# Sums over weights in a Strassen product: from four VectorE operations to two adding transfers and two additions in place

## The chip, the cores and the metric

The kernel runs on one core of one Trainium2 chip. The metric is device time in microseconds (us), from the start to the end of one execution; lower is better. Five engines work side by side, each through its own queue in order: TensorE (PE, with its weight loads as PEld), VectorE (DVE), ScalarE (ACT), GpSimd (POOL) and SyncE (SP), which here issues every DMA transfer.

## The reference

Two layers over 512 tokens of width 2048, in float32. The first layer is an mLSTM with 8 heads, the second an attention layer with 16 heads over one shared K and V. Nearly all of the work is in large products of a token matrix with a weight matrix:

```python
proj = h @ w_in                      # mLSTM: 2048 x 20496
y = sigmoid(o) * ht * silu(z)
x = x + gate * rmsnorm(y @ w_out)    # 4096 x 2048
kv = hkv @ kv_w                      # shared K and V: 2048 x 4096
qz = h @ w_in                        # attention: query and gate, 2048 x 4096
x = x + gate * rmsnorm((o * silu(z)) @ w_out)
```

## The kernel before, in words

A float32 product is made of three passes in the float32r type: each operand is split into a high and a low part, and `mm3` (L225) issues high x high, high x low and low x high. `split` (L180) makes the parts: ScalarE casts to the high part, VectorE subtracts to get the low part.

Weights come as a stream. `stream` (L60) lists the order in which the blocks of 128 x 128 are needed, and the host lays the array `wst` out in that order, in pieces of up to 1024 columns. `wpiece` (L187) takes the next piece: it loads it to a tile `wr` (tag `raw`, two buffers) and splits it to `wh` and `wl` (three buffers each).

Some products use Strassen's scheme in Winograd's form on 2 x 2 blocks of 128 x 128 weights and halves of 256 tokens: seven products of half width in place of eight. `proj_s` (L265) does this for two columns of weight blocks, c1 and c2. A pair of inner blocks k is either a Strassen pair (`sk`) or a plain one (`nk`); `pair_pieces` (L50) puts them into pieces, and `seven` and `eight` inside `proj_s` issue the matmuls. Strassen pairs of a piece form groups: one or two groups of one pair each, or (for the keys, `merged`) one group of two pairs. `proj_s` serves:

- the query, key and gate columns of heads 4 to 7 of the first layer (L584, up to 5 of 8 pairs, pool `hq`, three buffers of `wsh` and `wsl`),
- the shared keys (L928, 6 to 8 of 8 pairs, merged, pool `zp`, two buffers),
- the queries and gates of the 16 attention heads (L972, 7 of 8 pairs, pool `kq`, three buffers).

The sums over the weights are made in `wpiece` (L202 to L210). A piece carries for each group four blocks. VectorE subtracts twice into a tile `ws` (tag "ws", two buffers), and once in place into the raw tile (L206 to L208). Then the raw tile, with the sum that was made in place, is split as a whole, and each `ws` of three block widths is split to `wsh` and `wsl`. Of the seven products four read their weights from `wh` and `wl`, three from `wsh` and `wsl`.

The sums over the tokens are made by `half_sums` (L324), `three_sums` (L338) and at L948, and the four partial sums in PSUM (D, C, A, B) are combined at L313 to L322.

The order on each queue is not written out: the tile framework's planner orders the instructions by priority and by when it expects each to be ready, and puts in the waits for data and for buffers. `wpiece` runs with a priority 300 instructions ahead of its place (`ahead`, L184), so that loads and splits run ahead of the matmuls as far as the buffers allow. A tile of a tag with n buffers can be written once the tile n places back has had its last reader.

An attention head in its turn runs `queries` (L967): four pieces, of which the first holds one Strassen pair and the plain pair and the other three hold two Strassen pairs each, as two groups. Before the third piece, `mid` (L1039) issues the value product of the head two back and the scores and softmax of the head one back (`mixed` L1026, `weights` L987); after the last piece follow the transposes (`flipped` L1008).

Of the kernel before, what the change touches and what calls it, by code (L numbers as in the profile page):

```python
# [15 lines left out]
P = 128  # L16
# [43 lines left out]
def stream():  # L60
# [72 lines left out]
def hybrid_trunk(ctx, tc, xT, xN, c, adaT, cols, wst, wg, ext, kc, out):  # L133
# [53 lines left out]
    def wpiece(mat, groups=(), pl=None, bufs=2, tbufs=2):  # L187
# [7 lines left out]
        wpos[:] = i + 1, at + P * n  # L195
        with tc.high_priority(ahead[0]):
            own = spare[0] and i % (RAW_BUFS + 1) == 0
            raw = (spare[0] if own else wp).tile([P, 1024], F32, tag="raw", name=f"wr{i}", bufs=1 if own else RAW_BUFS)[:, :n]
            nc.sync.dma_start(raw, wst[at : at + P * n].rearrange("(p n) -> p n", p=P))
            ts = []  # L200
            c0 = 0
            for j, ns in enumerate(groups):  # L202
                w = ns * P
                r = raw[:, c0 : c0 + 4 * w]
                t = pl.tile([P, 3 * w], F32, tag="ws", name=f"ws{i}_{j}", bufs=tbufs)
                nc.vector.tensor_tensor(t[:, : 2 * w], r[:, w : 3 * w], r[:, : 2 * w], op=ALU.subtract)  # L206
                nc.vector.tensor_tensor(r[:, w : 2 * w], t[:, w : 2 * w], r[:, :w], op=ALU.add)
                nc.vector.tensor_tensor(t[:, 2 * w :], r[:, 3 * w :], r[:, w : 2 * w], op=ALU.subtract)  # L208
# [56 lines left out]
    def proj_s(mat, xs, ss, f, z1, z2, name, pl, bufs, at={}, merged=False):  # L265
# [6 lines left out]
        for i, (sk, nk) in enumerate(pieces):  # L272
# [10 lines left out]
            def eight():  # L283
                b0 = 4 * sum(len(ks) for ks in sk)
# [5 lines left out]
            def seven(g, ks):  # L290
                ns = len(ks)
                b0 = 4 * sum(len(u) for u in sk[:g])
# [861 lines left out]
```

## Time and profile before

| | |
|---|---|
| time, median of 2 runs | 2856.45 us (2855.57 to 2857.32) |
| span of the profiled execution | 2852.6 us |
| instructions in it | 40697 |
| granted TensorE clock, mean | 0.993 |
| DMA traffic | 524.61 MB, 184 GB/s on average |

For the profiled execution there is its span, from the first to the last instruction on the core; no separate time of that execution is listed, and the span lies 3.9 us below the median of the runs. Stretches of the span in which `proj_s` runs: about 890 to 1530 us (heads 4 to 7 of the first layer, with the value products between), 1980 to 2150 us (shared keys) and 2236 to 2640 us (attention).

In the rows of the profile, a name such as `wsh<-ws` gives the tile written and the tiles read; L181 and L182 are the two instructions of `split`, L223 is every matmul; `xN` is a count. In the table by stretches each engine has its busy time and, in brackets, its instructions. A line with `<-` after a number names what the engine waited for.

### The profile page before, as it was taken

What the parts mean: (1) busy time and instruction counts of PE and PEld (TensorE: products, weight loads), DVE (VectorE), ACT (ScalarE), POOL (GpSimd) and SP (SyncE); (2) the same over time, 40 slices, a digit from 0 to 9 for tenths busy, and PEclk for the clock granted to TensorE, in tenths of its full rate; (3) what the DMA queues carried; (4) which work ended last, traced back from release to release, by engine and by line L of the source; (5) the groups of instructions that cost most, each with busy time, mean ns of one, the idle gap of its engine ahead of it and who ended that gap; (6) DMA issues with size and microseconds to landing.
All of it is one profiled execution on the core that took longest, in us unless ns stands there. A gap on an engine that the chain in (4) does not pass through costs nothing.

```text
span 2852.6 us, 40697 instructions
## 1 busy us (share of the span) xinstructions
PE 2796.1 (98%) x15308; PEld 2425.8 (85%) x15308; DVE 2074.9 (73%) x3680; ACT 1337.4 (47%) x2005; POOL 0.2 (0%) x4
## 2 busy tenths in 40 slices
PE   7999999999999999999999999999999999999798
PEld 5787888888888989989898888888998999999687
DVE  7986978778688766857766445567875899998425
ACT  4244524234234544545545445577334566666323
POOL 0000000000000000000000000000000000000000
PEclk9999999999999999999999999999999999999899
DMA  8875687878764232332325657787336433333534
GB/s 298 301 245 185 232 308 247 296 236 279 260 236 132 93 115 97 108 100 100 104 96 168 205 197 241 232 285 259 137 137 210 141 126 117 121 126 123 184 104 173
DMA packets 177117, 524.61 MB, mean 184 GB/s; under 512 B 18788, under 2 KB 36228, under 8 KB 176408
## 3 DMA queue, kind: packets, MB, share of 16 engines
q1 hardware_dynamic: 176920, 522.01, 54.1%
q8 instruction: 120, 1.97, 0.3%
q14 instruction: 77, 0.63, 0.1%
HBM read 488.33 MB, written 38.85 MB: 185 GB/s over the span
## 4 chain that ended last, share of the span: by engine, by line
PE 86%; DVE 6%; DMA 4%; ACT 2%; issue 1%; SPq 0%; DVEq 0%; ACTq 0%
PE ps_y L223 18%; PE ps_v L223 10%; PE ps_o L223 5%; PE ps_z L223 5%; PE ps_azo L223 4%; PE ps_qk L223 4%; PE ps_kv L223 4%; PE ps_bzo L223 3%; PE ps_az L223 3%; PE ps_l L223 3%; PE ps_cz L223 2%; PE ps_dz L223 2%; PE ps_czo L223 2%; PE ps_dzo L223 2%; PE ps_s L223 2%; PE ps_bz L223 2%
## 5 line engine op out<-in xcount | busy, mean ns | idle before, releaser
L181 ACT CAST wh<-wr 128x1024 fp32r<-128x1024 f32 (+3 forms) x586 | 585.1, 1000 | 860.0 <-PE ps_y L223 210.0
L182 DVE TENSOR_TENSOR wl<-wr,wh 128x1024 fp32r<-128x1024 f32 (+3 forms) x586 | 678.5, 1160 | 421.5 <-ACT wh L181 416.7
L223 PE MATMUL ps_y<-wh,y 128*128 128x512 f32 x1536 | 478.6, 392 | 10.6 <-ACT wh L181 6.0
L223 PEld LDWEIGHTS ps_y<-wh,y 128*128 128x128 f32 x1536 | 289.9, 189 | 72.1 <-ACT wh L181 6.2
L223 PE MATMUL ps_v<-wh,h 128*128 128x512 f32 x1024 | 321.6, 390 | 0.4 <-DVE cv L529 0.4
L223 PE MATMUL ps_y<-wl,y 128*128 128x512 f32 x768 | 300.6, 391 | 0.0
L181 ACT CAST wsh<-ws 128x384 fp32r<-128x384 f32 (+1 forms) x253 | 138.4, 547 | 321.5 <-issue 127.3
L223 PEld LDWEIGHTS ps_v<-wh,h 128*128 128x128 f32 x1024 | 192.3, 188 | 40.5 <-issue 1.2
L182 DVE TENSOR_TENSOR wsl<-ws,wsh 128x384 fp32r<-128x384 f32 (+1 forms) x253 | 151.5, 599 | 99.8 <-ACT wsh L181 98.3
L223 PE MATMUL ps_v<-wl,h 128*128 128x512 f32 x512 | 199.8, 390 | 0.0
L381 DVE CUSTOM_DVE_ANT_0 ada<-ada,scB,cl 128x1024 f32<-128x1024 f32 x128 | 163.7, 1280 | 25.7 <-DMA ada<-in_adaT 25.6
L381 DVE CUSTOM_DVE_ANT_0 ada<-ada,scB,mod 128x1024 f32<-128x1024 f32 x128 | 163.9, 1280 | 19.9 <-DMA ada<-in_adaT 18.4
L223 PEld LDWEIGHTS ps_y<-wl,y 128*128 128x128 f32 x768 | 145.0, 189 | 30.6 <-DVE wl L182 0.9
L223 PE MATMUL ps_kv<-wh,hkv 128*128 128x512 f32 x512 | 159.3, 391 | 0.0
L206 DVE TENSOR_TENSOR ws<-wr 128x256 f32<-128x256 f32 (+1 forms) x253 | 112.2, 451 | 34.9 <-DMA wr<-in_wst 31.8
L223 PE MATMUL ps_qk<-h,wh 128*128 128x512 f32 x384 | 119.2, 390 | 0.0
L223 PE MATMUL ps_o<-h,wh 128*128 128x512 f32 x384 | 118.2, 389 | 0.0
L223 PE MATMUL ps_z<-h,wh 128*128 128x512 f32 x384 | 118.2, 389 | 0.0
L223 PEld LDWEIGHTS ps_v<-wl,h 128*128 128x128 f32 x512 | 96.2, 188 | 19.8 <-issue 0.9
L223 PEld LDWEIGHTS ps_kv<-wh,hkv 128*128 128x128 f32 x512 | 95.7, 188 | 19.5
L223 PE MATMUL ps_l<-h,wh 128*128 128x512 f32 x320 | 99.4, 392 | 1.3 <-ACT q L467 0.5
L223 PE MATMUL ps_kv<-wl,hkv 128*128 128x512 f32 x256 | 99.9, 390 | 0.1
(385 smaller groups left out, 5916.0 us busy)
## 6 DMA issues: line engine op xcount, KB each, us to landing
wr<-in_wst SPq DMA_DIRECT2D x520, 512.0 KB, 3.7
ada<-in_adaT SPq DMA_DIRECT2D x256, 512.0 KB, 5.9
xt<-nsc SPq DMA_DIRECT2D x46, 256.0 KB, 4.3
yr<-ysc SPq DMA_DIRECT2D x16, 512.0 KB, 4.3
wr<-in_wst SPq DMA_DIRECT2D x30, 256.0 KB, 4.0
wr<-in_wst SPq DMA_DIRECT2D x16, 384.0 KB, 5.8
bsc<-in_ext SPq DMA_DIRECT2D x16, 320.0 KB, 6.2
xt<-in_xT SPq DMA_DIRECT2D x4, 1024.0 KB, 7.0
```

Source lines behind the costliest of these rows:

```text
L181: nc.scalar.copy(hi, src)
L182: nc.vector.tensor_tensor(lo, src, hi.bitcast(F32), op=ALU.subtract)
L206: nc.vector.tensor_tensor(t[:, : 2 * w], r[:, w : 3 * w], r[:, : 2 * w], op=ALU.subtract)
L223: nc.tensor.matmul(ps, a, b, start=start, stop=stop)
L381: pin(nc.vector.tensor_tensor_reduce(at, at, scB[:, j * D // 2 : (j + 1) * D // 2], 1.0, mod[:, i : i + 1] if j else col(CB + i), ALU.mult ...
```

## The change

The sums are given other signs, so that all four over the weights are additions. A group's blocks in the stream are now three (0,c1), (1,c2), (1,c1), and the fourth, (0,c2), stands at the end of the piece. Two sums are made by transfers: a tile t (tag "ws") of two block widths gets the first two blocks by a load on SP's queue, and the fourth block is then added to both by a transfer with `accum_op` on GpSimd's queue, which reads it from the array twice. The piece itself is loaded without the fourth block. After the piece has been split, VectorE makes the other two sums by adding in place into the raw tile, and t and these two are split separately into the halves of one `wsh` and one `wsl` of four block widths. So three products read the piece's own blocks from `wh` and `wl`, and four read `wsh` and `wsl`. The buffers: `ws` has as many as `wsh` (three in the first layer, two for the keys and in attention, where before it had two everywhere), `wsl` at most two, and attention's `wsh` two for three. The sums over the tokens and the evacuation of PSUM change signs only.

```diff
     def tile_s(mat, c1, c2, f, merged=False):
         for sk, nk in pair_pieces(f, merged):
-            blocks = [(2 * k + i, c, P) for ks in sk for i, c in ((0, c1), (0, c2), (1, c2), (1, c1)) for k in ks]
-            out.append((mat, blocks + [(2 * k + i, c, P) for k in nk for i in range(2) for c in (c1, c2)]))
+            blocks = [(2 * k + i, c, P) for ks in sk for i, c in ((0, c1), (1, c2), (1, c1)) for k in ks]
+            blocks += [(2 * k + i, c, P) for k in nk for i in range(2) for c in (c1, c2)]
+            out.append((mat, blocks + [(2 * k, c2, P) for ks in sk for k in ks]))
...
-    def wpiece(mat, groups=(), pl=None, bufs=2, tbufs=2):
+    def wpiece(mat, groups=(), pl=None, bufs=2):
...
+        m = n - P * sum(groups)
         with tc.high_priority(ahead[0]):
             own = spare[0] and i % (RAW_BUFS + 1) == 0
-            raw = (spare[0] if own else wp).tile([P, 1024], F32, tag="raw", name=f"wr{i}", bufs=1 if own else RAW_BUFS)[:, :n]
-            nc.sync.dma_start(raw, wst[at : at + P * n].rearrange("(p n) -> p n", p=P))
+            raw = (spare[0] if own else wp).tile([P, 1024], F32, tag="raw", name=f"wr{i}", bufs=1 if own else RAW_BUFS)[:, :m]
+            src = wst[at : at + P * n].rearrange("(p n) -> p n", p=P)
             ts = []
-            c0 = 0
+            c0, c1 = 0, m
             for j, ns in enumerate(groups):
                 w = ns * P
-                r = raw[:, c0 : c0 + 4 * w]
-                t = pl.tile([P, 3 * w], F32, tag="ws", name=f"ws{i}_{j}", bufs=tbufs)
-                nc.vector.tensor_tensor(t[:, : 2 * w], r[:, w : 3 * w], r[:, : 2 * w], op=ALU.subtract)
-                nc.vector.tensor_tensor(r[:, w : 2 * w], t[:, w : 2 * w], r[:, :w], op=ALU.add)
-                nc.vector.tensor_tensor(t[:, 2 * w :], r[:, 3 * w :], r[:, w : 2 * w], op=ALU.subtract)
-                ts.append(t)
-                c0 += 4 * w
-            hi = wp.tile([P, 1024], F32R, tag="hi", name=f"wh{i}")[:, :n]
-            lo = wp.tile([P, 1024], F32R, tag="lo", name=f"wl{i}")[:, :n]
+                t = pl.tile([P, 2 * w], F32, tag="ws", name=f"ws{i}_{j}", bufs=bufs)
+                nc.sync.dma_start(t, src[:, c0 : c0 + 2 * w])
+                nc.gpsimd.dma_start(
+                    t.rearrange("p (a b) -> p a b", a=2),
+                    src[:, c1 : c1 + w].unsqueeze(1).to_broadcast([P, 2, w]),
+                    accum_op=ALU.add,
+                )
+                ts.append((t, raw[:, c0 + w : c0 + 3 * w]))
+                c0 += 3 * w
+                c1 += w
+            nc.sync.dma_start(raw, src[:, :m])
+            hi = wp.tile([P, 1024], F32R, tag="hi", name=f"wh{i}")[:, :m]
+            lo = wp.tile([P, 1024], F32R, tag="lo", name=f"wl{i}")[:, :m]
             split(hi, lo, raw)
             out = [(hi, lo)]
-            for j, t in enumerate(ts):
-                sh = pl.tile(list(t.shape), F32R, tag="wsh", name=f"wsh{i}_{j}", bufs=bufs)
-                sl = pl.tile(list(t.shape), F32R, tag="wsl", name=f"wsl{i}_{j}", bufs=bufs)
-                split(sh, sl, t)
+            for j, (t, r) in enumerate(ts):
+                w = groups[j] * P
+                nc.vector.tensor_tensor(r[:, :w], t[:, :w], r[:, :w], op=ALU.add)
+                nc.vector.tensor_tensor(r[:, w:], r[:, :w], r[:, w:], op=ALU.add)
+                sh = pl.tile([P, 4 * w], F32R, tag="wsh", name=f"wsh{i}_{j}", bufs=bufs)
+                sl = pl.tile([P, 4 * w], F32R, tag="wsl", name=f"wsl{i}_{j}", bufs=min(bufs, 2))
+                split(sh[:, : 2 * w], sl[:, : 2 * w], t)
+                split(sh[:, 2 * w :], sl[:, 2 * w :], r)
                 out.append((sh, sl))
         return out
...
-                    (D, h1_, 0, 1, lambda k: ss[k][1], False),
+                    (D, h1_, 1, 2, lambda k: ss[k][1], False),
                     (D, h0, 0, 0, lambda k: xs[2 * k][:, :, h0], end),
                     (C, h0, 1, 1, lambda k: ss[k][2], False),
                     (C, h1_, 1, 0, lambda k: ss[k][0], end),
-                    (A, h0, 0, 3, lambda k: xs[2 * k + 1][:, :, h0], False),
-                    (A, h1_, 1, 2, lambda k: xs[2 * k + 1][:, :, h1_], end),
-                    (B, h0, 0, 2, lambda k: ss[k][3], end),
+                    (A, h0, 0, 2, lambda k: xs[2 * k + 1][:, :, h0], False),
+                    (A, h1_, 1, 3, lambda k: xs[2 * k + 1][:, :, h1_], end),
+                    (B, h0, 0, 1, lambda k: ss[k][3], end),
...
-        proj_s("b_w_in", h2, h2s, ATT_PAIRS, z[:, 0:2, :], z[:, 2:4, :], f"z{h}", kq, 3, {2: mid})
+        proj_s("b_w_in", h2, h2s, ATT_PAIRS, z[:, 0:2, :], z[:, 2:4, :], f"z{h}", kq, 2, {2: mid})
```

The first product of `seven` (D, h1_) read the piece's split before; now it reads the group's.

More of the change, by code (lines that the diff above doesn't have):

```diff
@@ L283, in eight @@
             def eight():
-                b0 = 4 * sum(len(ks) for ks in sk)
+                b0 = 3 * sum(len(ks) for ks in sk)
                 for m, k in enumerate(nk):
@@ L327, in half_sums @@
         nc.vector.tensor_tensor(a11, a11, a21, op=ALU.subtract)
-        nc.vector.tensor_tensor(a21, a21, a22, op=ALU.add)
-        nc.vector.tensor_tensor(a22, a22, a11, op=ALU.subtract)
+        nc.vector.tensor_tensor(a21, a21, a22, op=ALU.subtract)
+        nc.vector.tensor_tensor(a22, a22, a11, op=ALU.add)
         nc.vector.tensor_tensor(a12, a12, a22, op=ALU.subtract)
@@ L341, in three_sums @@
         nc.vector.tensor_tensor(a11, a11, a21, op=ALU.subtract)
-        nc.vector.tensor_tensor(a22, a22, a11, op=ALU.subtract)
+        nc.vector.tensor_tensor(a22, a22, a11, op=ALU.add)
         nc.vector.tensor_tensor(a12, a12, a22, op=ALU.subtract)
@@ L947, in hybrid_trunk @@
         if k // 2 < ATT_PAIRS:
-            nc.vector.tensor_tensor(raw[0][:, 256:], raw[0][:, 256:], raw[1][:, 256:], op=ALU.add)
+            nc.vector.tensor_tensor(raw[0][:, 256:], raw[0][:, 256:], raw[1][:, 256:], op=ALU.subtract)
             h2s[k // 2][0] = h2[k][:, :, 256:]
```

8 lines of the change are left out of this document (4 added, 4 removed).

## The prediction

> **What bounds the kernel now.** I read the engine totals first, then the table by stretches of time, the chain that ended last, the waits, and the timeline of one attention head.
>
> ```profile
> span 2852.6 us, 40697 instructions
> PE 2796.1 (98%) x15308; PEld 2425.8 (85%) x15308; DVE 2074.9 (73%) x3680; ACT 1337.4 (47%) x2005; POOL 0.2 (0%) x4
> PE 86%; DVE 6%; DMA 4%; ACT 2%; issue 1%; SPq 0%; DVEq 0%; ACTq 0%
> ```
>
> PE is busy 98% of the span and makes 86% of the chain. The diff touches only the three stretches in which `proj_s` runs: gate and query/key projections of heads 4 to 7, the shared keys, the 16 attention heads. Columns: busy us and count of PE, PEld, DVE, ACT, POOL, granted clock, DMA share, GB/s.
>
> ```profile
> 890.00:1530.00 640.00, 636.68 (x3933) 575.58 (x3932) 455.38 (x861) 314.06 (x440) 0.00 (x0) 1.00 0.30 103
> 1980.00:2150.00 170.00, 165.45 (x1315) 162.33 (x1314) 135.90 (x225) 69.10 (x87) 0.00 (x0) 0.98 0.42 144
> 2250.00:2600.00 350.00, 348.75 (x2625) 333.23 (x2624) 317.61 (x843) 224.00 (x418) 0.00 (x0) 1.00 0.37 122
> ```
>
> PE stands still for 3.3, 4.6 and 1.3 us there: 9.2 us together. The change issues the same matmuls, so it cannot gain more than about 9 us (0.3%), whatever it takes off VectorE (DVE), which is 91% busy in the attention stretch but ends nothing there. The question is only what new waits it makes.
>
> The pace follows from two stretches of 50 us, one nearly all half-width products and one all of 512 columns:
>
> ```profile
> 2050.00:2100.00 50.00, 50.00 (x419) 50.00 (x418) 40.27 (x63) 18.44 (x22) 0.00 (x0) 1.00 0.38 137
> 2700.00:2750.00 50.00, 50.00 (x222) 41.40 (x221) 14.90 (x15) 13.20 (x19) 0.00 (x0) 1.00 0.34 119
> L313 ACT COPY z<-ps_dz x16: 358/366/375, 2255.3 to 2635.5; 128x256 f32<-128x256 f32 x16
> ```
>
> A half-width matmul takes 50/419 = 0.119 us, a full one 50/222 = 0.225. `seven` (21 half-width) is 2.5 us of PE and `eight` (12 full) 2.7. In attention, piece 0 (one Strassen group, one plain pair) is 5.2 us and pieces 1 to 3 (two groups each) 5.0. The evacuation of D marks heads: (2635.5-2255.3)/15 = 25.35 us each, for 7 groups; some 5 us are attention itself.
>
> **The change part by part.** *VectorE and ScalarE.* Rows of the attention stretch, by form (busy us, mean ns):
>
> ```profile
> L182 DVE TENSOR_TENSOR wl<-wr,wh 128x1024 fp32r<-128x1024 f32 x56 | 68.5, 1224 | 14.9 <-ACT wh L181 14.3
> L181 ACT CAST wh<-wr 128x1024 fp32r<-128x1024 f32 x56 | 58.6, 1046 | 36.4 <-DVE wr L207 34.8 <-DVE mx L1003 1.6
> L182 DVE TENSOR_TENSOR wsl<-ws,wsh 128x384 fp32r<-128x384 f32 x98 | 54.1, 553 | 9.0 <-ACT wsh L181 7.7
> L181 ACT CAST wsh<-ws 128x384 fp32r<-128x384 f32 x97 | 49.3, 508 | 51.9 <-PE ps_az L223 40.6 <-ACT z L313 8.0 <-DVE ws L206 1.8
> L206 DVE TENSOR_TENSOR ws<-wr 128x256 f32<-128x256 f32 x98 | 41.2, 421 | 1.2
> L208 DVE TENSOR_TENSOR ws<-wr 128x128 f32<-128x128 f32 x98 | 27.9, 285 | 0.9
> L207 DVE TENSOR_TENSOR wr<-ws,wr 128x128 f32<-128x128 f32 x97 | 27.0, 279 | 0.5
> L181 ACT CAST pt<-ps_t 128x256 fp32r<-128x256 f32 x13 | 5.1, 392 | 0.0
> ```
>
> Before, DVE spends per head 4 x 1.224 on the main split and 7 x (0.421 + 0.279 + 0.285 + 0.553) on groups: 15.7 us. After, the main split has 896 columns once and 768 three times (1.09 and 0.96 us, on the line between the 256- and 1024-column rows), and a group has two adds of 0.28 and two splits of 0.42: 4.0 + 9.8 = 13.8. That frees 1.9 us of DVE per head, 30 us in 16 heads, and is worth nothing, since DVE ends no PE wait of size there. ScalarE (ACT) gains instructions: 7 x 2 x 0.392 for 7 x 0.508, less on the main cast: about 1.2 us more per head, at 64% busy, costed at nothing; the main cast no longer waits for the sum in place (L207, 34.8 us above), a wait that PE does not see. If that cover were gone it would cost 19 us.
>
> The turned signs at the evacuation and in `half_sums` and `three_sums` keep every shape and count: nothing.
>
> *Traffic.* A pair now moves 7 blocks of 64 KB (2 in t, 2 added, 3 in raw) for 4: in attention 112 x 192 KB, about 54 GB/s on top of 122, with the DMA engines at a share of 0.37. SP issues one transfer more per group, at 0.33 us. Hidden by idle DMA engines and by a queue that mostly waits for slots; no price.
>
> *The new chain.* This is the term that counts. A tile t (tag ws) is now loaded, then added to by a second transfer that GpSimd (POOL) issues only once the load has landed, then read by the first add and by its split. Its slot is freed only then. In attention there are two slots for 7 groups a head, as there are now two for wsh and wsl instead of three. So a slot is used 3.5 times per head, and a head cannot be shorter than 3.5 C, with C the time from the issue of one load into a slot to that of the next. Behind the waiting load on SP stand the raw load of its piece, the next head's keys and values, the bias and the y2c store; behind POOL's transfer only the next addition; behind the add on DVE all of the softmax, for which the transposes and value products on PE wait.
>
> C is load + addition + work + hand-offs. Transfers and queues:
>
> ```profile
> wr<-in_wst SPq DMA_DIRECT2D x20, 128.0 KB, 2.6
> xt<-nsc SPq DMA_DIRECT2D x16, 128.0 KB, 4.7
> wr<-in_wst SPq DMA_DIRECT2D x30, 256.0 KB, 4.0
> wr<-in_wst SPq DMA_DIRECT2D x56, 512.0 KB, 3.3
> L961 SPq DMA_DIRECT2D kv<-ksc x16: 326/327/433, 2147.2 to 2599.3; - x16
> ```
>
> Start us, length us and engine of three casts and the subtractions that follow them:
>
> ```profile
> 2404.20 0.51 ACT L181 CAST wsh<-ws 128x384 fp32r<-128x384 f32 x1 [1.99 <-PE ps_az L223]
> 2405.13 0.55 DVE L182 TENSOR_TENSOR wsl<-ws,wsh 128x384 fp32r<-128x384 f32 x1
> ...
> 2406.72 0.52 ACT L181 CAST wsh<-ws 128x384 fp32r<-128x384 f32 x1 [0.49 <-ACT z L313]
> 2408.39 0.55 DVE L182 TENSOR_TENSOR wsl<-ws,wsh 128x384 fp32r<-128x384 f32 x1
> ...
> 2415.81 0.51 ACT L181 CAST wsh<-ws 128x384 fp32r<-128x384 f32 x1 [1.15 <-PE ps_az L223]
> 2416.35 0.56 DVE L182 TENSOR_TENSOR wsl<-ws,wsh 128x384 fp32r<-128x384 f32 x1 [0.59 <-ACT wsh L181]
> ```
>
> The load: 2.6 us, the row of 128 KB from the same array. Work: two adds and one split, 0.28 + 0.28 + 0.42 = 1.0. A hand-off to a busy in-order engine: the three casts end 0.42, 1.15 and 0.03 us before their subtraction starts, a half on average; two of them, 1.0. The addition: no row shows a transfer issued by POOL, nor one that adds. From below it takes what a plain load of as many bytes takes, 2.6; from above I bound it by the slowest load of 128 KB, 4.7. A gain is excluded. It moves two runs of 512 bytes per partition, reads both sides and is issued by software, so it is nearer the upper row: I take 4.0.
>
> C = 2.6 + 4.0 + 1.0 + 1.0 = 8.6; a head is 3.5 x 8.6 = 30.1 us for 25.35: 4.75 x 16 = **76 us**. With 2.6 for the addition C is 7.2 and a head 25.2: nothing. With 4.7, C is 9.3, a head 32.6: 115 us.
>
> The Trainium skill speaks for the lower end: "DMA: Bandwidth & Descriptors", section "Anatomy of one DMA — SWDGE (gpsimd) path", puts such a DMA at a fixed 2.0 us plus its bytes at 436 GB/s. By that the addition is an estimated 2.3 us, C 6.9, a head 24.2, and the sum would be no change; no run here shows it so far.
>
> *Two buffers of wsh for three.* The cast of a group now waits for PE's last read of the group two back. From there PE has 0.36 + 2.5 us of products before it needs the result; casts and subtractions of a group take about 2. Hidden by one group of PE work; with that gone, up to 0.5 us x 112 groups = 56 us, inside the range.
>
> *Shared keys.* 29 of the 32 groups are merged, with 256 KB per load; a slot is used every second piece, 10 us.
>
> ```profile
> L206 DVE TENSOR_TENSOR ws<-wr 128x512 f32<-128x512 f32 x29 | 19.9, 685 | 1.4 <-DMA wr<-in_wst 0.9 <-DVE zk L314 0.4
> ```
>
> C: load 4.0, addition 4.0, two adds of 256 columns and a split of 512 (0.42 + 0.42 + 0.68), hand-offs 1.0: 10.5. Over by 0.5 per two pieces: 29 x 0.25 = **7 us**, between 0 (addition 2.6) and 18 (4.7).
>
> *Heads 4 to 7 of the first layer.* 109 groups, three slots. Five groups take 3 x 5.2 + 5.0 = 20.6 us, so a slot has 12.4 us for C = 8.6. Hidden by 3.8 us of PE work per slot; with two slots it would be 2.5 x 8.6 = 21.5 us for every five groups, 0.9 us over, some 20 us in all.
>
> **Sum.** Against the profiled execution: 2852.6 + 76 + 7 = 2935.6. Its span lies 3.9 us under the median of the runs (2856.45), so the forecast is **2939.5 us**.
>
> **The rivals.**
>
> 1. *The chain is hidden (2857 us).* Place: the two slots of ws in attention. If the addition lands like a plain load, 3.5 C is at most 25.35, that is C at most 7.24, and PE sets the pace as before; the gain is at most 9 us. For it: 512 KB land in 3.3 us in that stretch, DMA engines are 63% idle, POOL does nothing else, and the 5 us of attention products per head let slots catch up. Against it: a two-group piece uses both slots in 5.0 us of PE, less than any C above, so each head has to catch up what three such pieces lose. The estimate from the Trainium skill above falls here.
>
> 2. *SP's order makes raw late (3002 us).* The program issues a piece's raw load behind its t loads. If the planner leaves it there, raw waits for the last slot of t as well: issue 0.33, raw 3.3, cast 0.83, subtraction 0.96, adds and splits of two groups 2.4, hand-offs 1.0 = 8.8 for each two-group piece, and 7.6 for piece 0: 34 us per head, 8.65 x 16 = 138, and 7 for the keys. For it: SP is one queue in order. Against it: DVE's work is interleaved instruction by instruction in the timeline, so the order follows expected readiness, and raw's slot frees earlier.
>
> 3. *VectorE holds POOL off (3025 us).* If making the addition's descriptors has to wait out one VectorE instruction, at most the 1.22 us of a main split, the addition is 5.2 us, C 9.8, a head 34.3: 143 us, and 25 in the keys.
>
> ```profile
> L1004 DVE TENSOR_SCALAR s<-s,mx 128x512 f32<-128x512 f32 x13 | 6.2, 480 | 0.0
> L1004 DVE TENSOR_SCALAR s<-s,mx 128x384 f32<-128x384 f32 x13 | 5.4, 414 | 0.0
> ```
>
> For it: DVE is 91% busy. Against it: only the scaling at L1004 runs at a faster rate per column (480-414 ns for 128 columns, 0.52 ns each, where the splits take (1224-421)/768 = 1.05), four short instructions a head.
>
> The Trainium skill ("SBUF — State Buffer", section "Who interferes with whom") says that a VectorE instruction in a 2-port mode shuts GpSimd out of writing descriptors, and infers that tensor_tensor does not. By that rule only L1004 could delay an addition, by under 0.5 us a head, 8 us in all; the trace before cannot show it.
>
> **How the numbers follow.** Chain exposed, my forecast: 0.48, of which 0.10 lies within 2% (addition under some 3.7 us). Hidden: 0.31. Raw late: 0.12. POOL held off: 0.08. A gain above 2% is excluded by the 9 us; 0.01 is left for it. About 2% is what a measurement of this kernel tells from no change. So faster 0.01, within 2% 0.31 + 0.10 = 0.41, slower 0.38 + 0.12 + 0.08 = 0.58. The forecast's own range is 2870 to 2990 (addition 3.0 to 4.7); taking in the hidden case below and the two dear ones above gives 2850 to 3030.
>
> **What would show it.** Right: heads in attention about 30 us apart at the evacuation of D; PE's idle time in the `proj_s` products with wsh or wh as operand, released by DVE splits, which in turn waited for a DMA into ws; 253 DMA issues on POOL landing in about 4 us; the first layer's heads unchanged near 640 us for their stretch; DVE some 30 us less busy in attention. Wrong: heads still at 25.35 us (rival 1); DVE waiting for wr rather than ws (rival 2); POOL's transfers much slower beside DVE's work than in gaps (rival 3); or PE losing its time in the first layer, where I see three slots as cover.

## The result and the profile after

The changed kernel takes 3099.68 us (median of 2 runs, 3094.99 to 3104.37), against 2856.45 before: a ratio of 1.0855, 95% interval 1.0835 to 1.0876. That is 243 us slower. The forecast was 83 us slower, so the sign was right and the size was a third of what came; the time lies above the range.

The page of the changed kernel: its span, engine totals, its two queues of data, and the chain that ended last, by engine and by line.

```profile
span 3093.2 us, 42385 instructions
PE 2877.2 (93%) x15308; PEld 2474.4 (80%) x15308; DVE 2000.0 (65%) x3680; ACT 1372.3 (44%) x2258; POOL 305.1 (10%) x257
q1 hardware_dynamic: 213352, 540.51, 53.4%
q0 software_dynamic: 68816, 36.98, 9.4%
PE 57%; DMA 21%; DVE 10%; issue 6%; ACT 5%; SPq 0%; POOLq 0%; ACTq 0%; DVEq 0%; POOL 0%
DMA ws<-in_wst 16%; PE ps_y L233 16%; PE ps_v L233 9%; PE ps_o L233 4%; PE ps_z L233 4%; PE ps_qk L233 3%; PE ps_kv L233 3%; PE ps_l L233 3%; DMA wr<-in_wst 3%; PE ps_azo L233 2%; DVE wl L183 2%; PE ps_lead L233 2%; DVE wsl L183 2%; PE ps_bzo L233 1%; ACT wh L182 1%
```

DVE lost 75 us of work in the whole kernel and PE fell from 98% busy to 93%. DMA, 4% of the chain before, is now 21% of it, and transfers into ws are 16%. The same three stages as stretches, each a little longer than before since it takes longer now (columns: length, busy and count of PE, PEld, DVE, ACT, POOL, clock, DMA share, GB/s):

```profile
890.00:1600.00 710.00, 668.31 (x3999) 591.99 (x3998) 432.55 (x875) 337.23 (x562) 127.59 (x106) 0.99 0.50 126
2050.00:2240.00 190.00, 167.03 (x1268) 161.95 (x1267) 115.01 (x210) 70.43 (x112) 33.72 (x28) 0.95 0.68 172
2330.00:2880.00 550.00, 448.86 (x2994) 413.62 (x2992) 335.09 (x960) 270.54 (x588) 130.15 (x108) 0.93 0.54 128
```

PE stands idle in all three, 42, 23 and 101 us, where it stood 1 to 5 us before. To see how much each stage costs I use the evacuations of D (L313 before, L323 after) as milestones, from the view of one source line (first and last start in us):

```profile
L323 ACT COPY zo<-ps_dzo x16: 365/373/373, 917.5 to 1579.2; 128x256 f32<-128x256 f32 x16
L323 ACT COPY z<-ps_dz x16: 366/372/376, 2351.1 to 2875.4; 128x256 f32<-128x256 f32 x16
L323 ACT COPY zk<-ps_dk x8: 349/367/369, 2062.3 to 2235.3; 128x256 f32<-128x256 f32 x8
```

Before, the rows of zo and zk are these; that of z stands in the prediction:

```profile
L313 ACT COPY zo<-ps_dzo x16: 373/373/373, 919.6 to 1524.2; 128x256 f32<-128x256 f32 x16
L313 ACT COPY zk<-ps_dk x8: 348/374/374, 2002.5 to 2146.0; 128x256 f32<-128x256 f32 x8
```

Up to the last zo the kernel is 55.0 us late; to the last zk another 34.3 (656.1 for 621.8 us from the one milestone to the other); from there to the last z another 150.6 (640.1 for 489.5). The three make 240 of the 240.6 us by which the span grew. A head of attention takes (2875.4 - 2351.1)/15 = 34.95 us, where 30.1 was forecast and 25.35 stood before.

The waits in attention (2330 to 2880 us; engine, line, waited for: total us, times, longest):

```profile
DVE wr L223 <- DMA ws<-in_wst: 129.0, 57, 5.3
ACT wsh L182 <- DMA ws<-in_wst: 97.1, 50, 6.7
ACT wh L182 <- DMA wr<-in_wst: 36.5, 27, 4.4
PE ps_dz L233 <- ACT wsh L182: 33.1, 24, 3.5
PE ps_dz L233 <- DVE wsl L183: 28.7, 25, 4.1
```

PE waits for the halves of the sums (wsh, wsl; 62 of its 101 us), and those wait for a DMA into ws. The raw tile (wr) is late too, but less. The transfers themselves, from issue to landing (KB each, median us):

```profile
ws<-in_wst SPq DMA_DIRECT2D x224, 128.0 KB, 2.5
ws<-in_wst POOLq DMA_DIRECT2D x224, 128.0 KB, 3.8
ws<-in_wst SPq DMA_DIRECT2D x29, 256.0 KB, 3.0
ws<-in_wst POOLq DMA_DIRECT2D x29, 256.0 KB, 4.9
```

So in the median the transfers of 128 KB cost what the prediction took for them, 2.5 and 3.8 us for 2.6 and 4.0; the mean of the additions in attention is 4.2. What is longer is the rest of a slot's round. I took from the trace, for each use of a slot of ws, the starts of its load, of its POOL transfer, of its first reader, the end of its last reader and the start of the next load into it (attention without its first head; medians need not add up):

| stage (slots) | load to POOL | POOL to first read | first read to release | release to next load | round |
|---|---|---|---|---|---|
| first layer (3), median | 3.07 | 5.41 | 6.46 | 0.07 | 15.54 |
| keys (2), mean | 4.03 | 5.94 | 2.52 | 0.05 | 12.54 |
| attention (2), mean | 3.25 | 4.33 | 2.40 | 0.03 | 10.01 |

In all three a slot is loaded again as soon as it is free, and so 3.5 x 10.01 is 35.0 us, the head. That would hold for any buffer that is refilled at once; that the slots set the pace in attention is told by the waits above and by the experiments. By position in a head the seven rounds in attention last 9.3, 10.0, 8.8, 8.3, 8.4, 12.9 and 12.4 us. Five are near the forecast's 8.6; the two of the last piece, next to the softmax, are 4 us longer. One of them, in lines from the timelines of SP, POOL and DVE (start, length, engine, line, operation, count, and in brackets the idle time before it and what ended it):

```profile
2503.52 5.28 SPq L207 DMA_DIRECT2D ws<-in_wst  x2
2507.25 1.20 POOL L208 DMA_DIRECT2D ws<-in_wst  x1 [4.07 <-DVE wr L224]
2511.11 0.29 DVE L223 TENSOR_TENSOR wr<-ws,wr 128x128 f32<-128x128 f32 x1 [1.53 <-issue]
2511.93 1.20 POOL L208 DMA_DIRECT2D ws<-in_wst  x1 [3.48 <-DVE mx L1011]
2517.89 0.29 DVE L223 TENSOR_TENSOR wr<-ws,wr 128x128 f32<-128x128 f32 x1 [3.72 <-DMA ws<-in_wst]
2518.10 1.09 DVE L183 TENSOR_TENSOR wl<-wr,wh 128x896 fp32r<-128x896 f32 x1
2519.10 0.42 DVE L183 TENSOR_TENSOR wsl<-ws,wsh 128x256 fp32r<-128x256 f32 x1
2519.55 0.33 SPq L207 DMA_DIRECT2D ws<-in_wst  x1
```

The first slot's load starts at 2503.52 (the line holds the second slot's load too, at 2508.47), its addition at 2507.25, its first reader at 2511.11. Its last reader is the split at 2519.10. That split stands on DVE behind the first add of the second slot (2517.89), and this add waits 3.72 us for the second slot's addition, issued at 2511.93. So one slot is held by the transfer into the other, and the next load goes out only at 2519.55: 16.0 us a round. In the last piece of a head this order of the two stands in 8 of 16 heads, in the second and third pieces in none. Where it stands, the round of the first slot averages 15.0 us; in the other heads 10.4.

### The profile page after: what moved, and what is told of

The parts are those of the page before. It is cut to its first block, busy times and chain, and to the rows that moved or that the text cites. A ratio compares the mean times of both kernels' runs of the same rounds, so it can differ in the third digit from the quotient of the medians.

```text
span 3093.2 us, 42385 instructions
## 1 busy us (share of the span) xinstructions
PE 2877.2 (93%) x15308; PEld 2474.4 (80%) x15308; DVE 2000.0 (65%) x3680; ACT 1372.3 (44%) x2258; POOL 305.1 (10%) x257
## 3 DMA queue, kind: packets, MB, share of 16 engines
q0 software_dynamic: 68816, 36.98, 9.4%
## 4 chain that ended last, share of the span: by engine, by line
PE 57%; DMA 21%; DVE 10%; issue 6%; ACT 5%; SPq 0%; POOLq 0%; ACTq 0%; DVEq 0%; POOL 0%
DMA ws<-in_wst 16%; PE ps_y L233 16%; PE ps_v L233 9%; PE ps_o L233 4%; PE ps_z L233 4%; PE ps_qk L233 3%; PE ps_kv L233 3%; PE ps_l L233 3%; DMA wr<-in_wst 3%; PE ps_azo L233 2%; DVE wl L183 2%; PE ps_lead L233 2%; DVE wsl L183 2%; PE ps_bzo L233 1%; ACT wh L182 1%
## 5 line engine op out<-in xcount | busy, mean ns | idle before, releaser
L183 DVE TENSOR_TENSOR wl<-wr,wh 128x1024 fp32r<-128x1024 f32 (+4 forms) x586 | 641.2, 1096 | 501.6 <-ACT wh L182 492.0
L182 ACT CAST wh<-wr 128x1024 fp32r<-128x1024 f32 (+4 forms) x586 | 554.9, 948 | 901.5 <-PE ps_y L233 207.9
L208 POOL DMA_DIRECT2D ws<-in_wst x253 | 304.9, 1213 | 2562.2 <-DVE h1r L338 875.8
L182 ACT CAST wsh<-ws 128x256 fp32r<-128x256 f32 (+1 forms) x253 | 108.6, 429 | 388.8 <-DMA ws<-in_wst 247.8
L223 DVE TENSOR_TENSOR wr<-ws,wr 128x128 f32<-128x128 f32 (+1 forms) x253 | 75.5, 304 | 222.8 <-DMA ws<-in_wst 155.9
L183 DVE TENSOR_TENSOR wsl<-ws,wsh 128x256 fp32r<-128x256 f32 (+1 forms) x253 | 114.1, 451 | 64.9 <-PE ps_azo L233 40.7
L182 ACT CAST wsh<-wr 128x256 fp32r<-128x256 f32 (+1 forms) x253 | 106.7, 427 | 101.2 <-DVE wr L224 100.4
L183 DVE TENSOR_TENSOR wsl<-wr,wsh 128x256 fp32r<-128x256 f32 (+1 forms) x253 | 114.1, 451 | 28.6 <-ACT wsh L182 25.7
```

The costliest lines, as they stand in the source:

```text
L182: nc.scalar.copy(hi, src)
L183: nc.vector.tensor_tensor(lo, src, hi.bitcast(F32), op=ALU.subtract)
L208: nc.gpsimd.dma_start(t.rearrange("p (a b) -> p a b", a=2), src[:, c1 : c1 + w].unsqueeze(1).to_broadcast([P, 2, w]), accum_op=ALU.add,)
L223: nc.vector.tensor_tensor(r[:, :w], t[:, :w], r[:, :w], op=ALU.add)
```

## The experiments

Three theories went into them. S: the round of a ws slot sets the pace (load, addition, reading), in attention and, against the prediction, also in the first layer and the keys. Q: SP's queue is held by t loads that wait for a slot, and what stands behind them is late. R: the raw tiles are held longer, as they wait for t, and the buffers of raw, wsh and wsl bind. One run each for the first eight, so that 10 us or less are not read from them; the later ones are medians of 4 or more runs. The kernel before took 2857.41 us beside the first four, 2851.41 beside the next four, then 2854.12 and 2854.88.

**1. No addition** (the transfer on POOL left out, and with it the fourth block of the sums):

```diff
-                nc.gpsimd.dma_start(
-                    t.rearrange("p (a b) -> p a b", a=2),
-                    src[:, c1 : c1 + w].unsqueeze(1).to_broadcast([P, 2, w]),
-                    accum_op=ALU.add,
-                )
```

> Leaves out the adding transfers on GpSimd's queue (so t is the plain blocks and the output is not the reference's); loads of t, buffers, order and all splits stay. Theory S (slots: load plus addition over two ws slots set the pace in attention, measured C about 10 us per use of a slot): C falls by the 4.6 us from the addition's issue to its first reader, to about 5.4, 3.5 x 5.4 = 19 us per head, under the 25.35 of PE, so attention returns to about 25.4 us per head and the whole to 2860 to 2880 us. Theory Q (SP's queue: raw loads stand behind t loads that wait for slots, and raw is held until its second split): the t loads stand where they stood, so the first layer and attention keep a good part of their loss, 2920 to 3000 us.

2880.19 us, at the upper end of S's band: 22.8 above before for 243 in the changed kernel. A head is 27.0 us, where S had 25.4. The loads of t stay on SP as they were, so Q alone doesn't explain the loss; nine tenths of it need the transfer on POOL.

**2. The sums on VectorE in the changed form** (t is made by one add from a raw tile that holds all four blocks; all buffers as in the changed kernel):

```diff
-                nc.sync.dma_start(t, src[:, c0 : c0 + 2 * w])
-                nc.gpsimd.dma_start(
...
-            nc.sync.dma_start(raw, src[:, :m])
+            nc.sync.dma_start(raw, src)
...
+                nc.vector.tensor_tensor(t.rearrange("p (a b) -> p a b", a=2), r0.rearrange("p (a b) -> p a b", a=2), x4.unsqueeze(1).to_broadcast([P, 2, w]), op=ALU.add)
```

> The added form without any transfer of its own: raw holds all four blocks again, VectorE makes the two sums of t by one addition of two block widths from raw, all else as in the changed kernel (two or three ws slots, wsl at most two, attention's wsh two, raw held until its second split). Theories S and Q: no t loads, no addition, so the time is back at 2855 to 2875 us. Theory R (fewer wsh and wsl buffers and a raw tile held longer are the cause): most of the 243 us stays, over 2950 us.

2868.72 us, within the band of S and Q: 11.3 above before, a head of 25.87 us:

```profile
L320 ACT COPY z<-ps_dz x16: 372/372/373, 2260.3 to 2648.4; 128x256 f32<-128x256 f32 x16
```

The form with additions, its signs, the separate splits and the fewer buffers cost little, some 11 us by this one run. R falls as the main cause.

**3. The load of t on POOL's queue too**, so that SP has none of it:

```diff
-                nc.sync.dma_start(t, src[:, c0 : c0 + 2 * w])
+                nc.gpsimd.dma_start(t, src[:, c0 : c0 + 2 * w])
```

> The loads of t go to GpSimd's queue ahead of their additions; SP has only the raw loads and the others. Theory Q: SP no longer stands at t loads, raw comes early, the 55 us lost in the first layer come back for the most part and attention gains too: at most 3060 us. Theory S: a load issued by GpSimd costs 1.2 us more and waits behind the addition before it, so C rises to 11.5 or more, a head to 40 us: about 3180 us, with the first layer no better.

3150.95 us, a head of 36.7, less than S's 3180 and 40. SP no longer waits for a slot of ws, and the kernel is slower by 51 us, not faster. In the first layer ACT's waits for raw fall from 67.9 to 35.1 us, and still the stage ends 62 us late for 55. So Q alone is not the cause. That moving the loads gained something and dearer slots took it away is not excluded, since t's loads now wait behind additions on POOL.

**4. Four slots of ws in attention:**

```diff
-                t = pl.tile([P, 2 * w], F32, tag="ws", name=f"ws{i}_{j}", bufs=bufs)
+                t = (wsp or pl).tile([P, 2 * w], F32, tag="ws", name=f"ws{i}_{j}", bufs=4 if wsp else bufs)
```

> In attention ws has four slots instead of two (in another pool); nothing else changes. Theory S: 7 uses over four slots are 1.75 x 10 = 17.5 us per head, under PE's 25.35, so most of attention's 154 us come back: 2940 to 2980 us, heads 25.5 to 28 us apart. Theory Q: loads of t still stand ahead of raw on SP, though they wait less: over 3020 us, heads above 30 us.

3004.57 us, above S's 2980 and below Q's 3020; a head falls from 34.95 to 28.24, just over S's band. The first layer and the keys stay where they were. Of the 150.6 us that attention had lost 57.9 are left, so S is right for the larger part, but not for all. In attention (2400 to 2760 us) the wait for the addition is gone from DVE, and ACT's cast of raw waits:

```profile
DVE wr L223 <- DMA ws<-in_wst: 1.0, 4, 0.4
...
ACT wh L182 <- DMA wr<-in_wst: 68.3, 47, 3.1
...
SPq L993 <- DVE mx L1013: 22.6, 13, 2.0
```

That looked like raw as the next bound, which 5, 6, 9 and 13 were to settle.

**5 and 6. A third raw buffer in attention**, with two slots of ws and with four. The room for it came from one buffer of the bias and one of the split queries, for two:

```diff
+    spare[0] = at
...
-        q = at.tile([P, 2, 384], F32R, tag="q", name=f"q{h}", bufs=2)
+        q = at.tile([P, 2, 384], F32R, tag="q", name=f"q{h}")
...
-        bias = at.tile([P, S], F32, tag="b", name=f"bias{h}", bufs=2)
+        bias = at.tile([P, S], F32, tag="b", name=f"bias{h}")
```

> In attention the raw pieces get a third buffer (room made by one buffer instead of two for the bias and for the split queries); ws keeps two slots. In the changed kernel both a ws slot and a raw buffer are loaded again 0.03 us after their release there, so either could be the bound. Theory S (ws slots): heads stay 33 to 35 us apart, 3065 to 3100 us. Theory R (two raw buffers, held 12 us until the last split of their sums): the use of a buffer, 17.5 us, is spread over three: 4 x 17.5 / 3 = 23 us per head, under PE's 25.35, about 2945 us.

> Both: four ws slots and a third raw buffer in attention. With four slots alone the head was 28.24 us and a raw buffer was used every 13.99 us, 4 x 13.99 / 2 = 28.0. If slots and raw buffers are the whole of it, the raw bound falls to 18.7 us per head and heads come to 25.4 to 26.5 us: 2955 to 2975 us. Theory O (the planner puts the reads of t too early in the queues of ScalarE and VectorE, which then stand still): little changes against four slots alone, 2990 to 3005 us.

3113.9 and 3054.5 us; heads of 36.1 and 31.4, both worse than without the third raw buffer. No expectation was met. With one bias buffer SP's bias load waits longer for the softmax than in 4 (37.6 us for 22.6 in 2400 to 2760 us), and what stands behind it on SP with it, so the one bias buffer might be the cause. 9 and 13 were to tell.

**7. POOL's transfer writes instead of adding** (t then holds the fourth block twice, not the sum):

```diff
-                    accum_op=ALU.add,
```

> GpSimd's transfer keeps its shape, its source and its waits but writes instead of adding (so t holds the fourth block alone and the output is not the reference's). If the software queue and the 512-byte runs are the price, it still lands in about 3.8 us and the time stays at 3080 to 3105 us. If the adding itself is, it lands in about 2.6 us, a slot's use in attention falls from 10.0 to 8.8 us, a head to 30.8, and the whole to 3020 to 3040 us.

3004.68 us: 153 above its before, where the changed kernel is 243 above. Neither case came: the landing lies between theirs and the time below both. The transfer of 128 KB lands in 3.1 us for 3.8, and it takes a fifth of the packets and half of the DMA engines' time for the same bytes (packets, MB, share). POOL is busy with an issue for 0.72 us (median; shortest and longest beside it, in ns), where one that adds takes 1.20, so about 0.5 of the 0.7 us go by on POOL:

```profile
q0 software_dynamic: 13072, 36.98, 4.5%
...
ws<-in_wst POOLq DMA_DIRECT2D x224, 128.0 KB, 3.1
...
L208 POOL DMA_DIRECT2D ws<-in_wst x253: 720/722/839, 878.2 to 2777.3; - x127
```

**8. Five slots of ws and two buffers of wsh in the first layer:**

```diff
-                t = pl.tile([P, 2 * w], F32, tag="ws", name=f"ws{i}_{j}", bufs=bufs)
+                t = pl.tile([P, 2 * w], F32, tag="ws", name=f"ws{i}_{j}", bufs=5 if bufs == 3 else bufs)
...
-                sh = pl.tile([P, 4 * w], F32R, tag="wsh", name=f"wsh{i}_{j}", bufs=bufs)
+                sh = pl.tile([P, 4 * w], F32R, tag="wsh", name=f"wsh{i}_{j}", bufs=min(bufs, 2))
```

> In heads 4 to 7 of the first layer ws has five slots instead of three (paid with two wsh buffers for three). Theory S: there too a slot is loaded 0.08 us after its release and used every 15.5 us in the median; over five slots that is 3.1 us per group, under the 4.1 of PE, so most of the 55 us lost there come back: 3045 to 3065 us. Theory R or O (raw buffers, used every 13.1 us there, or the order in the queues): 3085 to 3105 us.

3047.62 us, in S's band. The last zo comes at 1541.2 for 1579.2, 38 of the 55 us that this stage had lost; attention came out 12 us shorter in this run, though nothing was changed there.

```profile
L323 ACT COPY zo<-ps_dzo x16: 373/373/373, 915.6 to 1541.2; 128x256 f32<-128x256 f32 x16
```

Three slots are not cover in the first layer: S holds there too.

**9 and 13. The third raw buffer again**, with four slots of ws and both bias buffers; and its control, with one buffer of the split queries as in 9 but two raw buffers:

```diff
+            raw = (spare[0] if own else wp).tile([P, 896 if own and mat == "b_w_in" else 1024], F32, tag="raw", name=f"wr{i}", bufs=1 if own else RAW_BUFS)[:, :m]
...
-        q = at.tile([P, 2, 384], F32R, tag="q", name=f"q{h}", bufs=2)
+        q = at.tile([P, 2, 384], F32R, tag="q", name=f"q{h}")
```

> Attention alone: four ws slots as in the run with 3004.57 us, and a third raw buffer (896 columns) with both bias buffers kept and one query buffer. In the run with four slots a raw buffer was loaded again 14.0 us after its last load, two buffers for a head of 28.2 us (4 x 14.0 / 2). If raw is what binds there (R), three buffers bring the head to 25.4 to 26.5 us and the time to 2955 to 2975. If the head is held by the order of the queues, or by the slots still (O), it stays at 27.5 us or more and the time at 2990 or more.

> Control for the run with four slots and a third raw buffer in attention (3050.1 us, a head 30.9): the same four slots and one query buffer, but two raw buffers. If the third raw buffer did nothing or harm (O), this is at 3045 to 3060 or below 3045 with a head of 30.9 us or less, and raw is not what binds with four slots. If raw binds and the one query buffer hid its gain (R): above 3065, a head of 32 us or more.

9: 3050.12 us, ratio 1.0686 (1.0669 to 1.0703), a head of 30.9. 13: 3006.09 us, 1.0525 (1.0509 to 1.0540), a head of 28.6, which is the time of 4. So the query buffer costs nothing, and the third raw buffer itself costs 44 us; with both bias buffers the time is that of 6 within 5 us, so the bias buffer was not the cause there. Raw (R) is not what binds with four slots. With the third raw buffer, in 9, the cast of raw no longer waits, but DVE waits for the additions again (same stretch as under 4):

```profile
DVE wr L223 <- DMA ws<-in_wst: 56.5, 25, 3.6
...
SPq L994 <- DVE mx L1012: 39.2, 11, 7.0
```

In 4 the bias load on SP waited 22.6 us for the softmax, here 39.2, with t loads behind it; and a slot is held 8.7 us from its first reading to its release for 5.7, a round of 17.4 for 15.9. Times 7/4 that is 30.4 and 27.9 us, the head; but as a slot is refilled at once in both, this does not say that the slots bind. What grew is the time that a slot's readers hold it. Why they do so with an earlier raw was not tried by itself and stays open.

**10. More slots in all three stages** (four in attention, five in the first layer with two wsh, three for the keys):

```diff
-                t = pl.tile([P, 2 * w], F32, tag="ws", name=f"ws{i}_{j}", bufs=bufs)
+                t = (wsp or pl).tile([P, 2 * w], F32, tag="ws", name=f"ws{i}_{j}", bufs=4 if wsp else 5 if bufs == 3 else 3 if mat == "kv_w" else bufs)
```

> Only ws gets more slots: four in attention, five in the first layer (with two wsh there), three in the keys stage. If slots bind in each stage and the stages add up (S): the run with four slots in attention, 3004.6, less 52 for the first layer (as its run showed) and less 20 to 34 for the keys, 2918 to 2935; the keys stage takes 89 us after and 55 to 69 here. If the keys stage is held by the landing of its additions on one queue and not by its slots (O), it stays above 80 us and the time is 2945 or more.

2936.51 us, ratio 1.0291 (1.0275 to 1.0308): 82.4 above before, so slots give back 161 of 243 us. That is 1.5 us over S's bound and below O's:

```profile
L323 ACT COPY zo<-ps_dzo x16: 373/373/373, 913.9 to 1543.0; 128x256 f32<-128x256 f32 x16
L323 ACT COPY z<-ps_dz x16: 366/373/374, 2292.1 to 2711.9; 128x256 f32<-128x256 f32 x16
L323 ACT COPY zk<-ps_dk x8: 347/366/369, 2026.8 to 2166.5; 128x256 f32<-128x256 f32 x8
```

From the last zo to the last zk it takes 623.5 us for 621.8 before: one slot more gives back all that the keys lost, as S had it. (The 89 us in the expectation is how late the last zk is after the change, 55 of it from the first layer; here it is 20.5 us late.) The first layer is still 18.8 us late, and the stretch to the last z 55.9.

**11. The same with the third raw buffer** of 9:

> More slots in all three stages and the third raw buffer in attention. If slots and raw together make up the loss (S with R): 2870 to 2895, a head at 25.4 to 26.5 us. If the order of the queues keeps a part of it (O): 2905 or more. The kernel before is not beaten under either: at most 9 us of PE's idle time were left in these stages.

2981.0 us, ratio 1.0448 (1.0416 to 1.0480): O's case, and again 44 us worse for the third raw buffer.

**12. The kernel before with two buffers of wsh and wsl in attention:**

```diff
-        proj_s("b_w_in", h2, h2s, ATT_PAIRS, z[:, 0:2, :], z[:, 2:4, :], f"z{h}", kq, 3, {2: mid})
+        proj_s("b_w_in", h2, h2s, ATT_PAIRS, z[:, 0:2, :], z[:, 2:4, :], f"z{h}", kq, 2, {2: mid})
```

> The kernel before with two buffers each of ws, wsh and wsl in attention for three, nothing else changed. The prediction put the smaller number of buffers at nothing, hidden by a group of PE work: 2853 to 2862, a head 25.3 to 25.6 us. If the third buffer was cover that was needed (B): up to 0.5 us for each of 112 groups, 2870 to 2910, a head above 26 us.

2858.29 us, ratio 1.0012 (1.0004 to 1.0021), a head of 25.5: 4 us. Hidden, as predicted. (Of the three tiles that the expectation names, ws had two buffers before as well.)

**14 and 15. More slots as in 10, with POOL's transfers writing** (edit of 7), **and without them** (edit of 1):

> The kernel with more slots in all stages (2936.5 us) with POOL's transfers writing in place of adding; the sum is left out by that. With two and three slots the adding cost 95 us of time. If the length of the addition still paces with more slots (L): 2890 to 2905, about half of the 82 us that are left. If the slots hide it and the rest is from order and buffers (O): 2920 to 2940.

> The kernel with more slots in all stages and no transfer on POOL at all; the sum is left out by that. The kernel with few slots and no addition took 2880. If all that is left of the loss is the second transfer on the way to the slot (L): 2855 to 2875. If a good part is the split of the pair into two loads and the longer hold of the raw buffer (O): 2885 to 2920.

14: 2917.37 us, ratio 1.0216 (1.0199 to 1.0232). 15: 2878.11 us, 1.0079 (1.0062 to 1.0096). 14 lies below the band of O and well above that of L: the length of the adding is 20 of the 82 us that are left, no half. 15 comes 3 us above L's band and 7 below O's, so neither holds alone: most of the rest is the second transfer, and 23 us are not. In 15 attention has its pace again (its stretch, columns as above; a head of 25.8):

```profile
2265.00:2655.00 390.00, 382.75 (x2871) 366.05 (x2871) 322.48 (x928) 258.82 (x566) 0.00 (x0) 1.00 0.43 138
```

Set side by side, in us above the kernel before of the same group of runs (the lower two on the left are single runs):

| | slots as changed | more slots |
|---|---|---|
| POOL adds | 243.2 | 82.4 |
| POOL writes | 153.3 | 62.5 |
| no transfer on POOL | 22.8 | 23.2 |

Down a column, the adding is worth 90 us with few slots and 20 with more; the transfer apart from it 130 and 39. Across a row, slots are worth 161 us where the round is longest and nothing where there is no second transfer. That fits one chain per slot, with the slots as its cover. The bottom row, 23 us for two loads in place of one and the buffers, is not covered by slots; the runs don't split it further.

No version came below the kernel before. With PE idle for some 9 us in these stages before, none could by more than that.

## Why the prediction was right and wrong

**The mechanism was right for attention and the keys.** The chain of load, addition and reading through a slot sets the pace in attention; PE waits for DVE's and ACT's splits, those for a DMA into ws; the POOL transfers land in about 4 us. Runs 1, 4 and 10 show it by taking the addition or the scarcity of slots away. The time came 160 us over the forecast. By the milestones 55 of them are the first layer, where nothing was forecast, 75 attention (151 for 76) and 27 the keys (34 for 7).

**The addition.** Taken at 4.0 us between bounds of 2.6 and 4.7, it measured 3.8 in the median; in attention its mean is 4.2, and 5.4 for the last slot of a head, which is above the upper bound. The Trainium skill ("DMA: Bandwidth & Descriptors", section "Anatomy of one DMA — SWDGE (gpsimd) path") gave an estimated 2.3, on which the rival "hidden" leaned. The trace does not agree: 3.1 us when POOL's transfer only writes, 3.8 when it adds. It was right to place the value by the rows.

**Attention: the mis-sized term is "hand-offs 1.0".** C came out at 10.0 for 8.6. In the mean over the same rounds the load is 2.65 us, the addition 4.2 and the work 1.0, and the hand-offs are 2.15 where 1.0 was taken: 0.6 from the landing of the load to POOL's start, 0.15 from the landing of the addition to its first reader, 1.4 between the readers. Most of the excess is not an even delay: five rounds of a head average 8.9 us, two last 12.9 and 12.4. The prediction spoke of "behind the add on DVE all of the softmax", but took the reverse for granted, that the slots turn on while DVE does the softmax and one slot's split waits for nothing of the other slot. The timeline shows one way in which it fails: the split of the first slot stands behind the add of the second. It accounts for a part, since the order stands in half of the heads; the long additions of the last slot, 5.4 us where the other six positions have 3.5 to 4.4, are another, and why they are long was not tried. In all, C's excess is 3.5 x 1.4 = 4.9 us a head, 78 us in 16 heads; with the 76 forecast it makes 154, where the milestones show 151.

**The first layer: the step that failed.** "A slot has 12.4 us for C = 8.6", hidden by 3.8 us of PE work. A round took 15.5 us in the median. I took over C from attention. Here a slot is held 6.5 us from its first reader to its last, not the 1.0 of work, and its first reader starts 5.4 us after POOL's transfer for 4.3 in attention. In 77 of 106 groups the last reader is the split's subtraction on DVE, in the median 4.6 us after the cast. The waits of ACT and DVE in this stage (890 to 1600 us) show what holds these readers when the data is there:

```profile
ACT wsh L182 <- DMA ws<-in_wst: 80.0, 31, 5.6
ACT wh L182 <- DMA wr<-in_wst: 67.9, 41, 3.7
ACT wsh L182 <- DVE wr L224: 51.6, 39, 2.8
ACT wh L182 <- PE ps_v L233: 46.1, 15, 4.4
ACT wsh L182 <- PE ps_azo L233: 30.5, 16, 3.9
...
DVE wsl L183 <- PE ps_azo L233: 40.7, 25, 2.3
```

The cast waits for PE to give wsh back and for DVE's in-place sums, and casts of other pieces (wh) stand ahead of it; the subtraction waits for PE to give wsl back, of which the change left two buffers. So a slot can be held because the buffers that it is emptied into are still read by PE. Which of these holds it longest was not tried by itself; in run 8 the gain came with one buffer of wsh less. 55 us came where nothing was forecast; five slots took 36 to 38 of them away (8 and 10). "PE losing its time in the first layer" stood among the signs that would make the prediction wrong, and it did.

PE itself seldom waits for the sums there. Of its 42 us some 28 end with DVE's operations that read PSUM into zo and zq, 10 with wsl or wsh; the first three rows:

```profile
PE ps_n L233 <- DVE zo L740: 8.6, 4, 2.7
PE ps_azo L233 <- DVE zo L327: 8.4, 8, 2.1
PE ps_dzo L233 <- DVE wsl L183: 4.3, 8, 0.7
```

That those operations are late because splits that waited stand ahead of them on DVE fits the drop with five slots, but was not followed instruction by instruction.

**The keys.** C = 10.5 was forecast, 12.5 measured: the addition of 256 KB took 4.9 us for 4.0 in the median and 5.2 in the mean, since "4.0" was carried over from half the bytes. That is the larger part; the rest is 0.75 us from its landing to the first reader. Over by 2.5 us in two pieces, 29 x 1.25 makes 36 us, and the milestones show 34; a third slot took all of it back (10).

**Traffic, wsh, DVE.** "No price" for traffic is not contradicted: the DMA engines have a share of 0.54 in attention. 7 shows that the adding doubles the engines' time for its bytes; what that alone costs was not separated from the longer issue on POOL. Two buffers of wsh cost 4 us at most (12). The 30 us of DVE work forecast to be freed in attention came as 23 over fifteen heads (344.2 to 321.2 us), with 75 in the whole kernel, and bought nothing.

**The rivals.** "Hidden" is false; the load and the addition would have to fit 7.24 us, and five rounds of seven take 8.3 to 10.0. "SP's order makes raw late" is not the cause by itself: DVE and ACT wait for ws far more than for wr in attention, run 3 takes the t loads off SP and is slower, and a third raw buffer doesn't help (9, 13). (By the prediction's own rows its adds and splits of two groups are 2.8 us, not 2.4, which makes it some 20 us dearer.) Its 3002 us and the 3025 of the next rival were nearer to the result than my sum, by other ways. "VectorE holds POOL off" has no sign in POOL's own instructions (minimum, median, longest ns):

```profile
L208 POOL DMA_DIRECT2D ws<-in_wst x253: 1203/1203/2237, 876.2 to 2866.4; - x127
```

Half or more of them take the least time that any takes, with DVE 61% busy in attention. Nor do they land later: in attention the 46 additions issued while DVE was busy for over 80% of the issue landed in 4.2 us on average, the 25 with DVE busy for under 20% in 4.1. The Trainium skill's rule on 2-port instructions ("SBUF — State Buffer", section "Who interferes with whom") is not contradicted by that; no run here tests such instructions by themselves.

## What to carry to other kernels

When a transfer is put on the way to a tile that was made on an engine, count its buffers against the whole round from load to load: landing, the second queue's start, landing again, the wait for the first reader, and the time until the *last* reader, which in an engine that works in order can stand behind the reader of another slot. Take that last part from the stage itself, since a reader that must wait for its own output buffer holds its input as well. One or two slots more in each stage were worth more here (161 us) than a transfer that only writes (90).

## What the runs showed of the hardware

An adding transfer moves as 68816 packets what a writing one moves as 13072 (36.98 MB both), some 540 bytes a packet for 2830; in the traces the packets of data are of 512 bytes (1024 for the keys) against 4096. It takes 9.4% of 16 engines' span for 4.5%, and lands 0.7 us later at 128 KB as at 256 KB (4.9 for 4.2). An adding issue keeps POOL busy for 1.20 us and a writing one of the same shape for 0.72, where an issue takes SP 0.33.

The granted clock fell to 0.93 in attention, with PE idle for 101 of 550 us, and stood at 1.00 in the same stage with more slots and 34 us idle:

```profile
2285.00:2720.00 435.00, 401.39 (x2926) 376.09 (x2925) 327.14 (x941) 264.80 (x581) 125.29 (x104) 1.00 0.66 157
```

The stage whose PE stood idle more was clocked lower. Of the 240.6 us by which the span grew, 81 are PE busy for longer with the same 15308 matmuls (2877.2 for 2796.1 us; the profile models where a matmul ends). Between the first and the last z, with clocks of 1.00 before and 0.93 after:

```profile
2255.30:2635.50 380.20, 378.60 (x2846) 361.48 (x2845) 344.16 (x917) 244.61 (x462) 0.00 (x0) 1.00 0.37 121
2351.10:2875.40 524.30, 427.57 (x2846) 394.29 (x2846) 321.22 (x925) 261.22 (x566) 125.33 (x104) 0.93 0.54 127
```

The same 2846 matmuls take 49 us more there. Whether that lengthened the time, or filled what PE would have stood idle, was not tried by itself.
